# Two-source forms for VectorE's small operations, parameter rows set up at tile 8, splits written behind the products, output transposes at the end of the delta-net chain

## The chip, the cores and the metric

The kernel runs on one core of one Trainium2 chip. The metric is the device time of one execution in microseconds (us), as the median of some runs. Times inside a run are read from one profiled execution. Engines: PE is TensorE, DVE is VectorE, ACT is ScalarE, POOL is GpSimd, SP is SyncE (here it only issues DMAs).

## The reference, cut to what matters

One layer of a hybrid decoder on 256 tokens of width 1024 in float32, with 16 learned meta tokens ahead of them (272 positions):

```python
h = layer_norm(concat(meta, x))                   # 272 x 1024
proj = h @ w_in                                   # 1024 x 5640: q,k,v | z | beta, a | sb q,k,v | two gates of 1024
A = gated_delta_net(conv_silu(q, k, v), beta, g)  # 4 heads of 128, then rms_norm(o) * silu(z)
B = stick_breaking(sq, sk, sv)                    # 8 heads of 64
h = LN1(alpha*h + W_out(sig(gA)*W_A(A) + sig(gB)*W_B(B)))
h = LN2(alpha*h + HierMoE(h))                     # top-1 of 4 groups, top-2 of its 8 experts, FF 256
```

All of it is float32 in and out. The kernel writes each float32 matrix as a high and a low half (tiles of type fp32r) and makes three products of them.

## The kernel before, in words

**Stages.** To 24 us the embeddings are normalised and transposed; hTh and hTl (L213 to L217) are the halves of their transpose, `[128, 8, 272]`. From 15 to 235 us runs the projection with the two mixers woven into it. Then come the branch products, w_out, LN1 and the router (to about 323 us), then 32 experts whose weights stream from HBM (to about 525 us), and LN2.

**The projection.** `project` (L250) goes over 44 column tiles of w_in, each 128 columns wide. I number them 0 to 43 in the order of work. For each tile `load_split` (L224) issues a 512 KB DMA on SP (L231), ACT casts it to the high half (L232), and POOL subtracts to get the low half (L233; the *split*). For tiles 6, 8 and 10 (`DVE_SUB`) DVE does that. PE then makes 24 products (`mm3`, L237 to L239, 8 blocks of 3), and a `use` function takes the result out of PSUM (a convolution, a copy, a sigmoid gate). Raw tiles have a ring of WR = 3 buffers, split tiles one of WB = 3. Before the products of tile i, `project` writes the splits up to tile i+2 into the program.

**The chains.** While PE works through the tiles, `weave` (L63) advances other chains, written as generators, at given rates for each yield of `project` (4 yields a tile): masks; `delta_net` (the `gating` of L436, then two `local` parts, c = 0 and 1, and a meta part in turns, then `scan_state` for c = 0 and 1); `stick_breaking`; and `parameter_rows` (L824), which prepares the rows of gains and biases of the layer norms: four memsets and five affine selects on POOL (L828 to L835), 12 small DMAs on SP (L838), and operations on DVE and ACT that make `lnr`, `sel`, `RB` and `lnh` (L839 to L843). In the kernel before it waits 32 yields from tile 20 on, so it stands near tile 28 of the program. In the trace its POOL part runs at 184 us.

Inside `local`, `invert` computes the inverse of a triangular matrix by doubling: POOL makes masked copies mb4, mb8, ... of `mtf` (L488, one for each of c0, c1 and the meta part m), PE multiplies x4 = mb4 x pN, ACT casts the product to xo4 (L509), PE makes y4 and z4 from xo4 (L513, L516), DVE subtracts them. `scan_state(c)` ends in a short chain that normalises the output o: ACT squares (L710), DVE (L712 to L714), POOL a power (L715), DVE (L716), ACT scales (L718), and then PE transposes o to poT (L724), three yields after it. `pvp` (L685) is an earlier product of it that waits for DVE's vsc (L680).

**What sets the order.** PE and POOL run in exactly the order in which the program is written here. DVE, ACT and SP are put in order by a scheduler that reckons with its own times. Each engine runs its instructions strictly in that order; a waiting instruction holds up all that stand behind it.

After the projection its buffers become free, and only then do the first expert weights load (L889).

Of the kernel before, what the change touches and what calls it, by code (L numbers as in the profile page):

```python
# [78 lines left out]
def block_kernel(ctx: ExitStack, tc: tile.TileContext, io, out, dbg=None):  # L79
# [352 lines left out]
    def gating():  # L432
# [15 lines left out]
        V.tensor_scalar_add(beta, xin[:, 0, :], 1.0)  # L448
# [3 lines left out]
        V.tensor_scalar_add(zz, u, 2.0)  # L452
# [1155 lines left out]
```

## Time and profile before

| | us |
|---|---|
| median of 3 runs | 544.2 (541.4 to 544.8) |
| the profiled execution, own time | 538.66 |
| its span | 536.9 |
| mean granted TensorE clock over the span | 0.922 of full speed |
| PE busy | 463.5 (86%) |
| DVE, ACT, POOL busy | 238.2, 183.9, 172.7 |

The profiled execution is 5.5 us below the median of the three runs. Times "at 203 us" are counted from the start of its span. In the timeline a row is: start, duration, engine, line, operation, output<-input with shapes, count, and in brackets how long the engine had been idle and which engine's instruction ended that.

### The profile page before, as it was taken

The page shows a single profiled execution, that of the slowest core. Times are in us where ns is not written, and L with a number is a line of the kernel's source. Part 1 is how long each engine was busy: PE and PEld are TensorE (multiplying, and loading weights), DVE is VectorE, ACT ScalarE, POOL GpSimd, SP SyncE. Part 2 cuts the span into 40 slices and gives each one's busy share as a digit, 9 for nine tenths or more (in the row PEclk, how much of TensorE's full clock was granted, in tenths as well). Part 3 has the DMA queues.
Part 4 walks back from the last instruction along what each step waited for, and adds up shares of the span by engine and source line. Part 5 has one row for each costly group of instructions (what it writes and reads, how often), then busy time and mean ns, then how long its engine had stood idle before and what let it go on. Part 6 is the DMA issues. An engine that isn't in the chain of part 4 may idle for free. (4 is left out here: it accounts for less than half of the span.)

```text
span 536.9 us, 8673 instructions
## 1 busy us (share of the span) xinstructions
PE 463.5 (86%) x3301; PEld 328.6 (61%) x3301; DVE 238.2 (44%) x518; ACT 183.9 (34%) x382; POOL 172.7 (32%) x154
## 2 busy tenths in 40 slices
PE   7897999999999978997998888988879888667881
PEld 3697999999997877997876763533222222122330
DVE  5874645665296653039976736120220212110116
ACT  2453546436556365543443312120110202100310
POOL 6594698756544634738132100000000000000002
PEclk9697999999998997999999898889889898878886
DMA  8553344333441612797898958999999999999942
GB/s 210 126 151 86 79 117 109 89 92 108 117 110 49 159 42 78 207 305 270 306 338 336 399 234 336 419 418 418 419 420 420 417 419 418 417 415 419 410 196 79
DMA packets 74581, 136.33 MB, mean 254 GB/s; under 512 B 9857, under 2 KB 59154, under 8 KB 62242
## 3 DMA queue, kind: packets, MB, share of 16 engines
q1 hardware_dynamic: 72640, 134.26, 68.9%
q10 hardware_dynamic: 1890, 1.39, 0.8%
q8 instruction: 32, 0.52, 0.4%
q14 instruction: 19, 0.16, 0.1%
HBM read 133.54 MB, written 2.10 MB: 253 GB/s over the span
## 5 line engine op out<-in xcount | busy, mean ns | idle before, releaser
L233 POOL TENSOR_TENSOR ws_in<-wr_in,ws_in 128x1024 fp32r<-128x1024 f32 x41 | 99.4, 2429 | 64.6 <-ACT ws_in L232 64.3
L237 PE MATMUL pj<-hTh,ws_in 128*128 128x256 f32 (+1 forms) x352 | 109.3, 311 | 1.2 <-DVE hTh L213 0.7
L238 PE MATMUL pj<-hTl,ws_in 128*128 128x256 f32 (+1 forms) x352 | 103.1, 293 | 0.7 <-DVE hTl L217 0.7
L239 PE MATMUL pj<-hTh,ws_in 128*128 128x256 f32 (+1 forms) x352 | 102.6, 292 | 0.0
L1340 PE MATMUL pg<-gu,xs 128*32 128x512 f32 x640 | 77.6, 605 | 8.9 <-DMA gu<-expert_w_up 5.2
L1565 POOL TENSOR_SCALAR rs<-mv 128x1 f32<-128x1 f32 x2 | 0.4, 221 | 229.8 <-DVE mv L1564 229.8
L237 PEld LDWEIGHTS pj<-hTh,ws_in 128*128 128x128 f32 x352 | 69.2, 197 | 3.5 <-issue 1.0
L238 PEld LDWEIGHTS pj<-hTl,ws_in 128*128 128x128 f32 x352 | 69.3, 197 | 1.7 <-DVE hTl L217 1.7
L239 PEld LDWEIGHTS pj<-hTh,ws_in 128*128 128x128 f32 x352 | 69.1, 196 | 0.0
L1389 PE MATMUL py<-dn,hd 128*32 128x512 f32 x320 | 54.1, 802 | 11.9 <-DMA dn<-expert_w_down 6.9
L1340 PEld LDWEIGHTS pg<-gu,xs 128*32 128x32 f32 x640 | 31.0, 111 | 51.0 <-issue 45.5
L232 ACT CAST ws_in<-wr_in 128x1024 fp32r<-128x1024 f32 x44 | 45.9, 1044 | 3.0 <-DMA wr_in<-w_in 3.0
L1393 DVE TENSOR_TENSOR yy<-py,yy 128x512 fp32r<-128x512 f32 x20 | 13.8, 692 | 68.9 <-ACT yy L1392 61.7
L1365 DVE TENSOR_SCALAR sc<-pt,smod 128x256 fp32r<-128x256 f32 x10 | 4.8, 484 | 88.2 <-PE pt L1364 88.2
L1389 PEld LDWEIGHTS py<-dn,hd 128*32 128x32 f32 x320 | 13.2, 138 | 43.8 <-issue 27.2
L1401 PE MATMUL y<-yy,sc 128*128 128x512 f32 x80 | 24.5, 423 | 5.6 <-ACT yy L1392 3.0
L1392 ACT CAST yy<-py 128x512 fp32r<-128x512 f32 x20 | 11.7, 587 | 51.2 <-PE py L1389 51.2
L1401 PEld LDWEIGHTS y<-yy,sc 128*128 128x128 f32 x80 | 13.5, 188 | 22.7 <-ACT yy L1392 7.4
L1371 ACT ACTIVATE gs<-pg 128x256 f32<-128x256 f32 x10 | 3.8, 384 | 68.7 <-PE pg L1340 68.7
L314 DVE SCALAR_TENSOR_TENSOR qkv<-pj,cols,qkv 128x271 f32<-128x271 f32 (+2 forms) x36 | 17.9, 497 | 9.9 <-ACT qkv L312 9.2
L955 POOL TENSOR_TENSOR h<-h,gb 128x512 f32<-128x512 f32 x8 | 12.9, 1643 | 12.9 <-ACT gb L952 12.9
L771 DVE TENSOR_TENSOR_SCAN kp<-kp,one 128x144 f32<-128x144 f32 (+1 forms) x16 | 12.8, 842 | 7.2 <-ACT kp L766 7.2
(535 smaller groups left out, 806.6 us busy)
## 6 DMA issues: line engine op xcount, KB each, us to landing
gu<-expert_w_gate SPq DMA_DIRECT2D x32, 1024.0 KB
gu<-expert_w_up SPq DMA_DIRECT2D x32, 1024.0 KB
dn<-expert_w_down SPq DMA_DIRECT2D x32, 1024.0 KB
wr_in<-w_in SPq DMA_DIRECT2D x44, 512.0 KB
wr_o<-w_out SPq DMA_DIRECT2D x8, 512.0 KB
wr_w_branch_dn<-w_branch_dn SPq DMA_DIRECT2D x4, 512.0 KB
wr_w_branch_sb<-w_branch_sb SPq DMA_DIRECT2D x4, 512.0 KB
h<-x SPq DMA_DIRECT2D x2, 512.0 KB
```

The lines of the kernel that those rows point to most:

```text
L232: A.copy(wh, raw)
L233: (sub or V).tensor_sub(wl, raw, f32(wh))
L237: T.matmul(pt, lh, rh, start=first, stop=False)
L238: T.matmul(pt, lh, rl, start=False, stop=False)
L239: T.matmul(pt, ll, rh, start=False, stop=last)
L314: V.scalar_tensor_tensor(y[:, s:], pt[:, :L - s], ccol(3 - s, r + j), y[:, s:], op0=ALU.mult, op1=ALU.add)
L771: V.tensor_tensor_scan(k_, k_, bc(one1, [P, n]), 1.0, op0=ALU.mult, op1=ALU.mult)
L955: G.tensor_tensor(x_, x_, gb, op=op)
L1340: T.matmul(pgd[u, part][c, :], xsd[u, part][:, k, c], raw[e][0][:, :, k, :], start=k == 0, stop=k == KT - 1)
L1389: T.matmul(py[c, :], hd[(u + part) % 2][:, r, c], raw[e][1][:, r, n * 512:(n + 1) * 512], start=r == 0, stop=r == 1)
L1393: V.tensor_sub(yy[:, 1, :], py, f32(yy[:, 0, :]))
L1401: T.matmul(y[t][n], sct[(u + part) % 2][:, t * P:(t + 1) * P], yy[:, p_, :], start=False, stop=p_ == 1 and part == 0 and u == NQ - 1)
```

## The change

Four things change, and some small ones with them.

1. **Two-source forms.** Small DVE operations with one tensor source and a constant (`tensor_scalar`, `tensor_copy`) become `scalar_tensor_tensor` with a second tensor of zeros (or of a constant) through a helper `with_scalar`. This covers the six casts of hTh (L213), and operations on 128x9 or 128x4 elements in `gating`, `local`, `meta` and `scan_state`. Two copies (kTm, vTm) go to ACT. The tag `gtmp` gets three buffers in place of two.
2. **Parameter rows.** `parameter_rows` is started with the weave of tile 8 on, so that its memsets, selects and DMAs are written at tile 8; then it yields 100 times before the operations on DVE and ACT.
3. **Splits.** `project(i)` writes splits up to tile i+1 ahead of the products of tile i, and the split of tile i+2 behind the last product and the `use` of tile i.
4. **Output transposes.** poT and what follows it are taken out of `scan_state` and put into `out_turned(c)`, which runs for both c after the whole scan.

```diff
@@ prologue
+    def with_scalar(out, x, a, op):
+        V.scalar_tensor_tensor(out, x, a, bc(zero[:x.shape[0]], ...), op0=op, op1=ALU.add)
         if k % 4:
             A.activation(hf, pt[:, :L], AF.Identity, bias=bcol(k), scale=gcol(k))
-            V.tensor_copy(hTh[:, k, :], hf)
+            with_scalar(hTh[:, k, :], hf, 0.0, ALU.add)
@@ project
-            while len(split) < min(i + WB, len(todo)):
-                c = todo[len(split)][0]
-                split.append(load_split(...))
+            splits(i + WB - 1)
...
                 if k == KT - 1:
                     use(pt, j)
+                    splits(i + WB)
                     project.i += 1
@@ gating (and seven more of this kind)
-        V.tensor_scalar_add(beta, xin[:, 0, :], 1.0)
+        with_scalar(beta, xin[:, 0, :], 1.0, ALU.add)
@@ scan_state
         for h in range(HD):
             A.activation(o[:, h, :], o[:, h, :], AF.Copy, scale=sso[:, h:h + 1])
-        yield
-        yield
-        yield
+        os_.append(o)
+        yield
+    def out_turned(c):
+        o = os_[c]
         poT = v4(ps("gd", f"poT{c}"))
@@ delta_net
         for c in range(2):
             yield from scan_state(c, st, boxes[c])
+            yield
+        for c in range(2):
+            for _ in range(3):
+                yield
+            yield from out_turned(c)
@@ parameter_rows
-        for _ in range(32):
-            yield
         G.memset(f32(RB), 0.0)
...
+        for _ in range(100):
+            yield
         V.tensor_scalar(lnr, lnr, asc, None, op0=ALU.mult)
         A.copy(sel, self_)
@@ the weaves
+    prow = parameter_rows()
     weave(project(8), (mk, 0.375), (dn, R1))
-    weave(project(8), (dn, R1))
+    weave(project(8), (dn, R1), (prow, 1.0))
...
-    weave(project(20), (svc, 1.0), (dn, R3), (sbr, R4), (parameter_rows(), 1.0))
+    weave(project(20), (svc, 1.0), (dn, R3), (sbr, R4), (prow, 1.0))
+    drain(prow)
```

The lines of the kernel after are shifted: L232 and L233 become L243 and L244, L488 and L509 become L504 and L525, L715 becomes L731, L724 becomes L745, L841 becomes L867.

What this moves on the engines, at four places. First ACT, at tiles 11 to 13, before: `ws_in0` and `ws_in128` are the weights of tiles 12 and 13, `skT` copies of tiles 10 and 11, `pNc` and `xo4` belong to the inverse.

```order
L344 COPY skT_264<-pj2824_889 128x272
L232 CAST ws_in128_928<-wr_in128_927 128x1024
L500 CAST pNc1_868<-i0c1_921 128x512
L500 CAST pNm_880<-i0m_939 64x64
L509 CAST xo4c0_955<-x4c0_950 128x512
L509 CAST xo4c1_970<-x4c1_965 128x512
```

The same place on ACT after:

```order
L360 COPY skT_270<-pj2824_890 128x272
L243 CAST ws_in128_981<-wr_in128_980 128x1024
L516 CAST pNc1_869<-i0c1_927 128x512
L516 CAST pNm_886<-i0m_940 64x64
L866 CAST sel_99<-self__100 56x24
L525 CAST xo4c0_956<-x4c0_951 128x512
L525 CAST xo4c1_971<-x4c1_966 128x512
```

The scheduler has put the cast of `sel`, which reads POOL's `self_`, ahead of the casts xo4; `RB<-lnr` follows five rows later, ahead of the convolution of tile 12.

Second, POOL from the same tiles on, before (`ws_in2952` is the split of tile 11, `ws_in0` of 12, `ws_in128` of 13, `ws_in256` of 14).

```order
L233 TENSOR_TENSOR ws_in2952_819<-wr_in2952_818,ws_in2952_819 128x1024
L488 TENSOR_TENSOR mb4c0_859<-mtf0_812,off4_252 128x512
L488 TENSOR_TENSOR mb4c1_870<-mtf1_835,off4_252 128x512
L488 TENSOR_TENSOR mb4m_882<-mtfm_847,off4_252 64x64
L233 TENSOR_TENSOR ws_in0_885<-wr_in0_884,ws_in0_885 128x1024
L233 TENSOR_TENSOR ws_in128_928<-wr_in128_927,ws_in128_928 128x1024
L488 TENSOR_TENSOR mb8c0_948<-mtf0_812,off8_253 128x512
L488 TENSOR_TENSOR mb8c1_963<-mtf1_835,off8_253 128x512
L488 TENSOR_TENSOR mb8m_979<-mtfm_847,off8_253 64x64
L233 TENSOR_TENSOR ws_in256_986<-wr_in256_985,ws_in256_986 128x1024
```

POOL after (the row ahead of these is, in both, the second vs of L636):

```order
L504 TENSOR_TENSOR mb4c1_871<-mtf1_836,off4_258 128x512
L244 TENSOR_TENSOR ws_in2952_881<-wr_in2952_880,ws_in2952_881 128x1024
L504 TENSOR_TENSOR mb4m_888<-mtfm_848,off4_258 64x64
L244 TENSOR_TENSOR ws_in0_923<-wr_in0_922,ws_in0_923 128x1024
L504 TENSOR_TENSOR mb8c0_949<-mtf0_818,off8_259 128x512
L504 TENSOR_TENSOR mb8c1_964<-mtf1_836,off8_259 128x512
L244 TENSOR_TENSOR ws_in128_981<-wr_in128_980,ws_in128_981 128x1024
L504 TENSOR_TENSOR mb8m_985<-mtfm_848,off8_259 64x64
L852 MEMSET RB_96 56x256
L853 MEMSET self__100 56x24
L854 MEMSET lnr_97 56x256
L857 AFFINE_SELECT self__100<-self__100 56x24 x2
```

Each split has slipped behind one step of the inverse, and the rows' memsets and the selects that finish `self_` stand behind the split of tile 13 and mb8m.

Third, POOL near tile 29 (`ws_in3720`), before; `sso0` is the power of L715 for c = 0.

```order
L233 TENSOR_TENSOR ws_in3592_1899<-wr_in3592_1898,ws_in3592_1899 128x1024
L233 TENSOR_TENSOR ws_in3720_1986<-wr_in3720_1985,ws_in3720_1986 128x1024
L715 TENSOR_TENSOR sso0_2033<-sso0_2033,mhalf_114 128x4
L233 TENSOR_TENSOR ws_in3848_2060<-wr_in3848_2059,ws_in3848_2060 128x1024
L233 TENSOR_TENSOR ws_in3976_2104<-wr_in3976_2103,ws_in3976_2104 128x1024
```

and after:

```order
L244 TENSOR_TENSOR ws_in3592_1998<-wr_in3592_1997,ws_in3592_1998 128x1024
L731 TENSOR_TENSOR sso0_2065<-sso0_2065,mhalf_120 128x4
L244 TENSOR_TENSOR ws_in3720_2092<-wr_in3720_2091,ws_in3720_2092 128x1024
L244 TENSOR_TENSOR ws_in3848_2136<-wr_in3848_2135,ws_in3848_2136 128x1024
L244 TENSOR_TENSOR ws_in3976_2204<-wr_in3976_2203,ws_in3976_2204 128x1024
```

The split of tile 29 now stands behind the power of c = 0; before, it stood ahead of it.

Fourth, PE around the two transposes poT before (`pj3720` is tile 29, `pj4488` tile 35, `pz4` and `po2` belong to the stick-breaking chain).

```order
L239 MATMUL pj3720_2108<-hTh_175,ws_in3720_1986 128x256
L724 MATMUL poT0_2127<-ident_105,o0_1970 128x128 x4
L759 MATMUL pz4_2136<-skT_264,sqT_263 128x144
...
L239 MATMUL pj4488_2494<-hTh_175,ws_in4488_2358 128x256
L724 MATMUL poT1_2507<-ident_105,o1_2345 128x128 x4
L800 MATMUL po2_2516<-wT4_2457,sv0_265 64x256
```

and after (`pj4872` is tile 38):

```order
L250 MATMUL pj4488_2481<-hTh_181,ws_in4488_2428 128x256
L745 MATMUL poT0_2494<-ident_105,o0_2007 128x128 x4
L826 MATMUL po2_2503<-wT4_2444,sv0_271 64x256
...
L250 MATMUL pj4872_2627<-hTh_181,ws_in4872_2579 128x256
L745 MATMUL poT1_2640<-ident_105,o1_2276 128x128 x4
L248 MATMUL pj4872_2627<-hTh_181,ws_in4872_2579 128x256
```

The transpose of c = 0 stands six tiles later, that of c = 1 three tiles later.

## Rows read from the trace of the kernel before

**Rows 1.** The page: busy time by engine (share of the span, instructions).

```profile
PE 463.5 (86%) x3301; PEld 328.6 (61%) x3301; DVE 238.2 (44%) x518; ACT 183.9 (34%) x382; POOL 172.7 (32%) x154
```

**Rows 2.** Busy time by engine in stretches: start:end, length, busy (and instructions) of PE, of PE's weight loads, DVE, ACT, POOL, then the granted TensorE clock as a share of full speed, the DMA's share and GB/s.

```profile
130.00:150.00 20.00, 20.00 (x164) 18.61 (x163) 7.53 (x16) 11.89 (x28) 10.01 (x6) 1.00 0.42 110
150.00:225.00 75.00, 67.94 (x538) 60.70 (x537) 41.67 (x75) 39.81 (x93) 37.56 (x25) 0.93 0.37 96
325.00:500.00 175.00, 142.57 (x984) 51.24 (x987) 29.32 (x80) 25.48 (x58) 0.00 (x0) 0.88 1.01 418
```

**Rows 3.** What PE waited for over the whole run: its line, whom it waited for, us in total, times, the longest.

```profile
PE poT L724 <- ACT o L718: 5.8, 2, 4.6
...
PE pdc L469 <- DVE gg L464: 3.4, 1, 3.4
...
PE pvp L685 <- DVE vsc L680: 1.2, 1, 1.2
```

**Rows 4.** Stretches around those waits, columns as in rows 2.

```profile
47.40:53.30 5.90, 5.76 (x27) 5.72 (x28) 1.70 (x5) 1.56 (x4) 0.99 (x1) 0.50 0.30 86
...
166.60:167.90 1.30, 0.09 (x2) 0.06 (x1) 0.76 (x1) 0.51 (x2) 0.74 (x1) 1.00 0.00 0
...
169.70:173.00 3.30, 3.30 (x17) 2.55 (x16) 2.50 (x3) 3.20 (x8) 2.25 (x1) 0.52 0.27 81
...
180.00:182.00 2.00, 0.75 (x7) 0.55 (x5) 2.00 (x7) 1.41 (x2) 0.83 (x2) 1.00 0.18 16
198.40:203.00 4.60, 0.05 (x1) 0.00 (x0) 3.17 (x6) 1.59 (x6) 3.32 (x2) 1.00 0.00 0
...
203.80:210.60 6.80, 6.80 (x36) 5.43 (x37) 3.09 (x3) 3.18 (x7) 2.35 (x1) 0.51 0.56 151
```

**Rows 5.** The timeline of POOL, DVE, ACT and PE ahead of the transpose for c = 1.

```profile
199.20 1.02 POOL L715 TENSOR_TENSOR sso<-sso,mhalf 128x4 f32<-128x4 f32 x1 [6.92 <-ACT wT L788]
200.20 2.33 POOL L233 TENSOR_TENSOR ws_in<-wr_in,ws_in 128x1024 fp32r<-128x1024 f32 x1
200.25 2.30 DVE L716 TENSOR_TENSOR sso<-sso,rq 128x4 f32<-128x4 f32 x1 [1.01 <-POOL sso L715]
...
202.59 1.28 ACT L718 ACTIVATE o<-o,sso 128x128 f32<-128x128 f32 x4 [3.01 <-DVE sso L716]
203.04 1.35 PE L724 MATMUL poT<-ident,o 128*128 128x128 f32 x4 [4.59 <-ACT o L718]
```

**Rows 6.** The timeline around the power for c = 0: POOL's split of tile 29 and the power, PE's first product of tile 29; between them all scans of the stick-breaking chain on DVE, with columns as in rows 7 (the longest begins at 155.6).

```profile
155.39 2.81 POOL L233 TENSOR_TENSOR ws_in<-wr_in,ws_in 128x1024 fp32r<-128x1024 f32 x1 [2.91 <-ACT ws_in L232]
...
L771 DVE TENSOR_TENSOR_SCAN kp<-kp,one x16: 443/692/2836, 146.8 to 194.1; 128x144 f32<-128x144 f32 x8, 128x272 f32<-128x272 f32 x8
...
163.98 1.01 POOL L715 TENSOR_TENSOR sso<-sso,mhalf 128x4 f32<-128x4 f32 x1 [5.79 <-DVE sso L714]
...
164.34 0.28 PE L237 MATMUL pj<-hTh,ws_in 128*128 128x256 f32 x1
```

**Rows 7.** DVE beside POOL: the casts of hTh and the subtractions of hTl (durations in ns: least, median, longest; first and last start), and then the timeline row of beta.

```profile
L213 DVE CAST hTh<-hf x6: 294/296/2443, 16.1 to 21.8; 128x272 fp32r<-128x272 f32 x6
...
L217 DVE TENSOR_TENSOR hTl<-hf,hTh x8: 431/440/1267, 14.9 to 22.4; 128x272 fp32r<-128x272 f32 x8
...
42.07 0.94 DVE L448 TENSOR_SCALAR beta<-xin 128x9 f32<-128x9 f32 x1 [2.48 <-ACT xin L446]
```

**Rows 8.** The timeline of POOL from the second `vs` on (the split at 64.11 is that of tile 11, the two at 71.67 are those of tiles 12 and 13), then that of the rows' POOL part.

```profile
62.14 2.04 POOL L636 TENSOR_TENSOR vs<-ssk,half 128x4 f32<-128x4 f32 x2 [3.10 <-DVE ssk L631]
64.11 2.73 POOL L233 TENSOR_TENSOR ws_in<-wr_in,ws_in 128x1024 fp32r<-128x1024 f32 x1
66.81 4.63 POOL L488 TENSOR_TENSOR mb4c<-mtf,off 128x512 fp32r<-128x512 f32 x2
...
71.67 4.73 POOL L233 TENSOR_TENSOR ws_in<-wr_in,ws_in 128x1024 fp32r<-128x1024 f32 x2
76.36 2.53 POOL L488 TENSOR_TENSOR mb8c<-mtf,off 128x512 fp32r<-128x512 f32 x2
78.84 0.33 POOL L488 TENSOR_TENSOR mb8m<-mtfm,off 64x64 fp32r<-64x64 f32 x1
...
184.05 0.31 POOL L828 MEMSET RB<- 56x256 f32 x1
...
184.66 0.47 POOL L833 TENSOR_SCALAR_AFFINE_SELECT self__100<-self__100 56x24 f32<-56x24 f32 x2
```

**Rows 9.** The timeline of PE and ACT at the first step of the inverse (the first row is PE's first product of tile 11), and of SP's small DMAs of the rows (first and last) and DVE's row that follows them.

```profile
70.75 0.37 PE L237 MATMUL pj<-hTh,ws_in 128*128 128x272 f32 x1
...
73.31 0.59 ACT L509 CAST xo4c<-x4c 128x512 fp32r<-128x512 f32 x1 [0.81 <-PE x4c L507]
...
76.25 0.56 PE L513 MATMUL y4c<-xo4c,pTc 128*128 128x128 f32 x4
...
84.26 0.56 PE L513 MATMUL y8c<-xo8c,pTc 128*128 128x128 f32 x4
...
184.69 0.69 SPq L838 DMA_DIRECT2D lnr<-ln_g  x2
...
188.97 0.64 SPq L838 DMA_DIRECT2D lnr<-ln_emb_b  x2
...
195.96 0.34 DVE L839 TENSOR_SCALAR lnr<-lnr,asc 56x256 f32<-56x256 f32 x1
```

More of the change, by code (lines that the diff above doesn't have):

```diff
@@ L138, in block_kernel @@
     V.memset(one1, 1.0)
+    zero = ht.tile([P, 1], F32, name="zero")
+    V.memset(zero, 0.0)
+    pcol = ht.tile([P, 1], F32, name="pcol")
+    V.memset(pcol, float(P))
+    ecol = ht.tile([P, 1], F32, name="ecol")
+    V.memset(ecol, RMS_EPS)
+    def with_scalar(out, x, a, op):
+        V.scalar_tensor_tensor(out, x, a, bc(zero[:x.shape[0]], list(x.shape)) if len(x.shape) == 2 else bc(zero[:x.shape[0], :, None], list(x.shape)), op0=op, op1=ALU.add)
     half = ht.tile([P, HD], F32, name="half")
@@ L245, in columns, with splits @@
         todo.extend((c0 + j * P, n0, use, j) for j in range(n // P))
+    def splits(n):
+        while len(split) < min(n, len(todo)):
+            c = todo[len(split)][0]
+            split.append(load_split(w_in[:, :, c:c + P], f"in{c}", sub=V if len(split) in DVE_SUB else G))
     def project(n):
@@ L250, in project @@
             i = project.i
-            while len(split) < min(i + WB, len(todo)):
-                c = todo[len(split)][0]
-                split.append(load_split(w_in[:, :, c:c + P], f"in{c}", sub=V if len(split) in DVE_SUB else G))
+            splits(i + WB - 1)
             c, n0, use, j = todo[i]
@@ L438, in gating @@
         xin = mx.tile([P, 3, 9], F32, name="xin")
-        V.tensor_scalar_mul(xin[:, 0, :], bb, -1.0)
+        with_scalar(xin[:, 0, :], bb, -1.0, ALU.mult)
         V.scalar_tensor_tensor(xin[:, 1, :], aa, -1.0, aa, op0=ALU.mult, op1=ALU.min)
@@ L447, in gating @@
         u, eal = xin[:, 1, :], xin[:, 2, :]
[L448 removed]
+        with_scalar(beta, xin[:, 0, :], 1.0, ALU.add)
         V.reciprocal(beta, beta)
         zz = mx.tile([P, 9], F32, name="zz")
[L452 removed]
+        with_scalar(zz, u, 2.0, ALU.add)
         V.reciprocal(zz, zz)
@@ L457, in gating @@
         poly = mx.tile([P, 9], F32, name="poly")
-        V.tensor_scalar_mul(poly, z2, 1.0 / 17.0)
+        with_scalar(poly, z2, 1.0 / 17.0, ALU.mult)
         for d in (15, 13, 11, 9, 7, 5, 3):
@@ L461, in gating @@
         V.scalar_tensor_tensor(poly, poly, 1.0, zz, op0=ALU.add, op1=ALU.mult)
-        V.tensor_scalar_mul(poly, poly, 2.0)
+        with_scalar(poly, poly, 2.0, ALU.mult)
         V.scalar_tensor_tensor(poly, aa, 0.0, poly, op0=ALU.max, op1=ALU.add)
@@ L474, in gating @@
         A.activation(decm, pdc[:64, 24:25], AF.Exp)
-        V.tensor_scalar_mul(nedec, dec[:, 0, :], -1.0)
+        with_scalar(nedec, dec[:, 0, :], -1.0, ALU.mult)
         yield
@@ L544, in meta @@
         vTm = mx.tile([P, 64], F32, name="vTm")
-        V.tensor_copy(kTm.rearrange("p (h t) -> p h t", h=HD), qkv[:, 4:8, :NM])
+        A.copy(kTm.rearrange("p (h t) -> p h t", h=HD), qkv[:, 4:8, :NM])
         yield
@@ L551, in meta @@
         vsm = mx.tile([64, 1], F32, name="vsm")
-        V.tensor_scalar_add(ssm, ssm, RMS_EPS)
+        with_scalar(ssm, ssm, RMS_EPS, ALU.add)
         G.tensor_tensor(vsm, ssm, half[:64, :1], op=ALU.pow)
@@ L583, in meta @@
             yield "idle"
-        V.tensor_copy(vTm.rearrange("p (h t) -> p h t", h=HD), qkv[:, 8:12, :NM])
+        A.copy(vTm.rearrange("p (h t) -> p h t", h=HD), qkv[:, 8:12, :NM])
         yield
@@ L607, in local @@
         tag = ("gd", "sb")[c]
-        Aall = mx.tile([P, HD, P], F32, name=f"Aall{c}", tag="gtmp", bufs=2)
+        Aall = mx.tile([P, HD, P], F32, name=f"Aall{c}", tag="gtmp", bufs=3)
         gc = gg[:, 4 * c:4 * c + 4]
@@ L617, in local @@
         A.activation(E, pD, AF.Exp)
-        Es = mx.tile([P, HD, P], F32, name=f"Es{c}", tag="gtmp", bufs=2)
+        Es = mx.tile([P, HD, P], F32, name=f"Es{c}", tag="gtmp", bufs=3)
         V.tensor_mul(Es, E, bc(lt_[:, None, :], [P, HD, P]))
@@ L630, in local @@
             V.tensor_mul(kd, pk, bc(esuf(c)[:, :, None], [P, HD, P]))
-        V.tensor_scalar_add(ssk, ssk, RMS_EPS)
+        with_scalar(ssk, ssk, RMS_EPS, ALU.add)
         s = mx.tile([P, HD], F32, name=f"s{c}")
@@ L655, in local @@
             A.activation(junk(), pq[:, h, :], AF.Square, accum_out=rq[:, h:h + 1])
-        V.tensor_scalar(rq, rq, RMS_EPS, float(P), op0=ALU.add, op1=ALU.mult)
+        V.scalar_tensor_tensor(rq, rq, RMS_EPS, bc(pcol, [P, HD]), op0=ALU.add, op1=ALU.mult)
         G.tensor_tensor(rq, rq, mhalf, op=ALU.pow)
@@ L691, in scan_state @@
             T.matmul(pqS[:, h, :], qT(h)[:, tok], St[:, h, :], start=True, stop=True)
-        o = mx.tile([P, HD, P], F32, name=f"o{c}", tag="gtmp", bufs=2)
+        o = mx.tile([P, HD, P], F32, name=f"o{c}", tag="gtmp", bufs=3)
         for h in range(HD):
@@ L713, in scan_state @@
         V.tensor_mul(sso, sso, rq)
-        V.tensor_scalar(sso, sso, 1.0 / P, RMS_EPS, op0=ALU.mult, op1=ALU.add)
+        V.scalar_tensor_tensor(sso, sso, 1.0 / P, bc(ecol, [P, HD]), op0=ALU.mult, op1=ALU.add)
         G.tensor_tensor(sso, sso, mhalf, op=ALU.pow)
@@ L718, in scan_state @@
             A.activation(o[:, h, :], o[:, h, :], AF.Copy, scale=sso[:, h:h + 1])
+        os_.append(o)
         yield
-        yield
-        yield
+    os_ = []
+    def out_turned(c):
+        o = os_[c]
         poT = v4(ps("gd", f"poT{c}"))
@@ L724, in scan_state @@
             T.transpose(poT[:, h, :], o[:, h, :], ident)
-        of = mx.tile([P, HD, P], F32, name=f"of{c}", tag="gtmp", bufs=2)
+        of = mx.tile([P, HD, P], F32, name=f"of{c}", tag="gtmp", bufs=3)
         V.tensor_mul(of, poT, zT[:, :, c * P:(c + 1) * P])
```

## The prediction

> **What bounds the kernel now.** I read the page's busy times first. PE is busy for 86% of the span and no other engine for more than 44% [rows 1]. The table by stretches tells where that holds: in quiet tiles of the projection PE is busy all the time at full clock; from 150 to 225 us it is idle for 7 us and its granted clock is 0.93; from 325 to 500 us the DMA's share is 1.01 at 418 GB/s and PE has time over [rows 2]. So the projection is bound by PE and its waits, and the experts by HBM. The change touches the projection. The experts' weights can only load when the projection's buffers are free, so I carry a microsecond won or lost in the projection to the end one for one.
>
> The list of PE's waits then names what can be won: two waits at the output transposes poT (4.6 and 1.2 us), one of 1.2 us at pvp, and one of 3.4 us at pdc, in the gating [rows 3]. A wait costs more than its length. After the 4.6 us from 198.4 on, PE worked for 6.8 us at a granted clock of 0.51, the lower level (1.2 of 2.4 GHz); after the 1.3 us at 166.6 it had 0.52 for 3.3 us; after the wait at pdc 0.50 for 5.9 us. After the wait at pvp the stretch to 182 shows 1.00 [rows 4]. So the price of the clock is 0.49 x 6.8 = 3.3 us, 0.48 x 3.3 = 1.6 us, 0.50 x 5.9 = 2.9 us, and nothing.
>
> **Output transposes.** Ahead of poT for c = 1 stands a chain: the power on POOL, 1.02 us; then DVE's L716, a product of 128x4 elements that takes 2.30 us because it starts beside a split of 2.33 us and ends with it; then ACT's scaling, and PE [rows 5]. None of this gets shorter, but PE now asks for it six tiles later (c = 0) and three tiles later (c = 1). A quiet tile takes 24 x 20.0 / 164 = 2.9 us [rows 2], so three give 8.8 us, more than the 4.6 us missing. I take both waits as gone with their clock: 4.6 + 3.3 + 1.2 + 1.6 = 10.7 us. The transposes and the work behind them on DVE and ACT stay. The wait at pvp came of vsc standing behind other work on DVE; pkS for c = 1, which feeds it, moves ahead of the scores pz, so I take its 1.2 us as won too (bounds 0 and 1.2). Gain: 11.9 us.
>
> **Two-source forms.** L716 has two sources in SBUF and was held for a whole split [rows 5]. The single-source cast of hTh was held too (2443 ns where the median is 296), and so was beta with its one tensor (0.94 us) [rows 7]. The rows give no reason for one form to escape where the other does not. So beta stays late, and the wait at pdc of 3.4 us with it, which in any case follows the exponentials on ACT. I take 0 there; if the form did escape, up to 0.8 us of beta. In the prologue the six casts of 0.295 us become operations like the subtraction of hTl, 0.44 us [rows 7]: +0.15 us each, 0.9 us on DVE, which PE follows closely in tile 0; I take +0.6 us, with bounds of -2.1 (the long cast is freed, 2.44 - 0.3) and +0.9.
>
> The Trainium skill, page "SBUF — State Buffer", section "Who interferes with whom", states that a DVE instruction with two SBUF inputs contends with a GpSimd instruction that reads SBUF, and that the shared port pair is an exclusive lock held for the whole instruction. L716 agrees: 2.30 us beside a split of 2.33. By that rule the edit goes the wrong way: each new form that meets a split where the old one did not would wait for up to 2.3 us. By the rows above the old forms were held already, so my sum has no such term.
>
> **Parameter rows.** This is the largest loss. In ACT's new order the cast of sel stands ahead of the casts xo4, and it waits for POOL's self_. On POOL the memsets and selects stand behind both mb4c, the splits of tiles 11, 12 and 13, mb4m, mb8c and mb8m. POOL had no idle time from 62.14 to 79.17 us [rows 8], and the same work in another sequence ends at the same time, about 79.2. Then come the memsets and the selects of self_: from 184.05 to 184.66 + 0.47 they took 1.08 us [rows 8]. So self_ is ready at about 80.3. The bounds are 78.1 (both mb4c as quick as mb8c, 2.1 us less) and 81.4 (one more step slow by as much as half a split). Then come sel, which is small (I put 0.2 us), and xo4 with 0.59 us [rows 9]: PE can start y4c at 81.1. It asked for it at 76.25 [rows 9], and a little later in the new kernel, since tile 11 is late: 76.5. PE waits 4.6 us (2.4 to 5.7). Nothing else stands in PE's order that it could do first. The clock should fall as after the waits of 3.4 and 4.6 us: +2.9 us, or 1.6 after the shortest. Loss: 7.5 us (4.0 to 9.0).
>
> Later on ACT the cast RB waits for DVE's row on lnr, and that for the 12 small DMAs on SP. They can start after the memset of lnr, about 80, and their issue took 184.69 to 189.61, 4.9 us [rows 9]. The last lands between that and DVE's row at 195.96, 6.3 us later [rows 9]; I take 2 us, nearer to the short end since DVE had other work ahead of that row. That is 87, when PE, late itself, is just finishing tile 12: no further wait. Where they stood before, PE did not wait for them, so nothing is won there. SP is held for those 4.9 us; the weights of tile 17 behind them are wanted more than ten us later.
>
> **Splits.** The split of tile 11 goes behind both mb4c: instead of 64.11 to 66.84 it runs from 68.7 to 71.1 or 71.5 [rows 8], and PE's first product of tile 11 was at 70.75 [rows 9]; the low half is needed by the third product. +0.4 us (0 to 0.8).
>
> The split of tile 29 ended at 158.2; now it stands behind the power for c = 0, which started at 163.98, while PE starts tile 29 at 164.34 [rows 6]. By these times the split ends at 163.98 + 1.01 + 2.3 = 167.3 and PE waits 2.8 us. But the split used to hold a scan on DVE in that chain for 2.84 us where the median is 0.69 [rows 6]: without it the power comes up to 2.1 us earlier, and the wait is 0.7. I take 1.4 us, in between but nearer to the short one, and 0.8 us of clock by half of the 1.6 behind the 1.3 us wait (0 to 1.6). Loss 2.2 us (0.7 to 4.4). The wait for poT of c = 0 that stood 2 us later is then simply replaced. The power of c = 1 now stands ahead of the split of tile 34, two full tiles or 5.8 us behind the product that its chain follows, with other products between; the power and the split take 3.4 us of it [rows 5], so I expect no wait.
>
> **Sum.** -11.9 + 0.6 + 7.5 + 0.4 + 2.2 = -1.2 us, so the profiled execution of 538.66 us becomes about 537.5. That one lies 5.5 us below the median of 544.2, and I take the difference over as it is: 543.0 us. Within 1% (5.4 us) is about what a measurement of this kernel can tell from no change. Own range of this case: with the bounds of the two large losses, 538.0 to 546.7.
>
> **Rivals.**
> - *sel is ready in time, so only the gains stay.* If the POOL work ahead of it shrinks, or ACT's wait falls where PE has other work, the 7.5 us go: 543.0 - 7.5 = 535.5 us. For it: mb4c took 4.63 us where mb8c of the same shape took 2.53, so POOL can be quicker here. Against: even that leaves 2.4 us of wait and a loss of 4.0, giving 539.5, and POOL shows no gap. Half the loss together with no wait at tile 29 gives 537.3, faster by over 1%.
> - *The rows make PE wait twice.* If the small DMAs land 6.3 us after their issue, DVE's row on lnr ends at 91.6, RB at 92.0, and behind it on ACT stand the convolution of tile 12, the cast of tile 15 and xo8, three operations of at least 0.59 us like xo4, some 2.1 us: 94.1. PE reached y8c 8.0 us after y4c (84.26 against 76.25) [rows 9], with the lower clock behind the wait about 11: 92.2. It waits 2 us, with 1.6 us of clock: 546.6 us. It decides from a landing of about 4.4 us on; each us later costs one more. With the upper ends of sel (+1.5) and of tile 29 (+2.2) it passes 549.6, slower by over 1%. For it: the order in which these stand; against: small transfers on a DMA that is less than half used in this stage.
> - *Two-source forms escape POOL's splits.* The long cast and beta run free, up to 0.8 + 2.1 + 0.6 = 3.5 us: 539.5. Against it is L716.
> - *The change does not remove the poT waits*, because something else of the delta-net chain ends as late: 543.0 + 7.9 = 550.9. Against: nothing in PE's order between tiles 31 and 38 needs that chain but poT.
>
> **How the numbers follow.** My case 0.45; sel in time or nearly so 0.27; rows twice 0.13; two-source forms 0.08; poT waits stay 0.07. Faster by over 1% (below 538.8): most of the second, a third of the fourth, a little of mine, 0.32. Slower by over 1%: half of the third, nearly all of the fifth, a little of mine, 0.18. Same: 0.50. The range of 8 in 10 leaves out the ends: 533 to 551.
>
> **What would show it.** After the change the list of waits has no poT row, and the stretch near 204 to 210 shows full clock. There is a new wait of 4 to 5 us at y4c for ACT's xo4, ACT idle ahead of sel for POOL's self_ near 80 us, and a granted clock of 0.5 behind it. There is a wait of 1 to 3 us at tile 29's second product for POOL's split. Beta still takes over 0.5 us, and pdc waits over 2.5 us. I am wrong if y4c waits less than 2 us, if another wait of over 3 us appears, or if the projection's end moves by more than 4 us.

## The result and the profile after

| | before | after |
|---|---|---|
| median of 20 runs, us | 540.4 (538.4 to 544.8) | 545.6 (542.5 to 553.7) |
| ratio, 95% interval | | 1.0103 (1.008 to 1.0126) |
| span of the profiled execution | 536.9 | 544.1 |

With more runs the median of before is 540.4, not the 544.2 of the first three; ratios below are against runs of before on the same chip. One run of the changed kernel, 553.7 us, lies far above the others and is not in the ratio. The kernel became 1% slower where I forecast 0.2% faster: a small miss in size, but the sign was wrong, and two of my terms, the transpose for c = 1 and the prologue, were far out. That 545.6 lies within 0.5% of my 543.0 is luck in part: my number stood on the 544.2, and with the same sum on 540.4 it would have been 539.2.

PE's waits after, as in [rows 3] (its line, whom it waited for, us in total, times, longest):

```profile
PE y4c L529 <- ACT xo4c L525: 4.0, 1, 4.0
...
PE pdc L485 <- DVE gg L480: 3.9, 1, 3.9
...
PE po L831 <- DVE wTm L816: 3.8, 1, 3.8
...
PE pj L250 <- POOL ws_in L244: 1.6, 2, 1.1
```

The poT waits are gone, y4c is there with about the length forecast (4.0 us for 4.6), and there is one of over 3 us that I had not named: po. To see what each costs with its clock, take the start of each tile's first product from PE's timeline and subtract that of before. The steps in this shift are the terms of the sum. Each row is from one profiled execution, in us:

| tile | 3 | 8 | 12 | 13 | 14 | 29 | 30 | 35 | 36 | 43 | end of span |
|---|---|---|---|---|---|---|---|---|---|---|---|
| after, us | 2.8 | 3.8 | 4.5 | 12.5 | 13.1 | 13.0 | 11.6 | 9.5 | 7.3 | 8.2 | 7.2 |
| rows back | 1.9 | 2.7 | 3.5 | 3.5 | 3.4 | 3.5 | 2.0 | -0.1 | -7.4 | -7.2 | -8.0 |
| wTm on ACT | 2.6 | 3.6 | 4.3 | 12.5 | 12.9 | 12.9 | 11.4 | 9.3 | 1.5 | 1.9 | 3.4 |
| product c = 1 on POOL | 1.8 | 2.5 | 3.2 | 10.3 | 10.7 | 10.6 | 9.2 | 7.1 | 2.9 | 3.2 | 2.3 |
| sel on POOL | 2.8 | 2.2 | 2.9 | 2.9 | 10.0 | 10.9 | 9.4 | 7.3 | 4.3 | 5.1 | 4.1 |
| transposes back | 2.5 | 1.9 | 2.6 | 9.5 | 9.8 | 9.8 | 7.8 | 11.4 | 8.2 | 8.0 | 9.9 |
| transposes alone | 1.2 | 1.7 | 1.7 | 1.7 | 1.7 | 1.7 | -1.1 | 3.9 | -3.9 | -3.8 | -1.6 |
| rows alone | 1.2 | 0.1 | 0.1 | 0.1 | 4.9 | 7.1 | 5.7 | 13.1 | 11.6 | 12.3 | 12.2 |
| late splits alone | 1.1 | 2.0 | 2.7 | 2.7 | 2.7 | 2.7 | 0.8 | 1.2 | -1.3 | -1.6 | -2.0 |
| best | 1.5 | 2.0 | 2.0 | 2.0 | 2.0 | 2.0 | -0.9 | -2.7 | -10.5 | -10.4 | -8.4 |

(The lower rows belong to the experiments; "back" is one part of the changed kernel undone, "alone" one part on the kernel before.) The first place is tiles 11 to 13. The timeline of POOL and ACT after, which answers to [rows 8, 9]:

```profile
70.49 2.61 POOL L504 TENSOR_TENSOR mb4c<-mtf,off 128x512 fp32r<-128x512 f32 x1 [0.76 <-DVE mtf L660]
73.06 2.38 POOL L244 TENSOR_TENSOR ws_in<-wr_in,ws_in 128x1024 fp32r<-128x1024 f32 x1
...
80.49 2.34 POOL L244 TENSOR_TENSOR ws_in<-wr_in,ws_in 128x1024 fp32r<-128x1024 f32 x1
82.79 0.31 POOL L504 TENSOR_TENSOR mb8m<-mtfm,off 64x64 fp32r<-64x64 f32 x1
83.05 0.30 POOL L852 MEMSET RB<- 56x256 f32 x1
...
83.66 0.47 POOL L857 TENSOR_SCALAR_AFFINE_SELECT self__100<-self__100 56x24 f32<-56x24 f32 x2
...
84.15 0.21 ACT L866 CAST sel<-self__100 56x24 fp32r<-56x24 f32 x1 [7.48 <-POOL self__100 L857]
84.27 1.06 ACT L525 CAST xo4c<-x4c 128x512 fp32r<-128x512 f32 x2
```

ACT stands still for 7.48 us ahead of a cast of 0.21 us, and xo4 stands behind it. The second place is the chain that ends at po, in order of time:

```profile
196.79 1.02 POOL L731 TENSOR_TENSOR sso<-sso,mhalf 128x4 f32<-128x4 f32 x1 [4.71 <-ACT osh L834]
197.76 2.38 POOL L244 TENSOR_TENSOR ws_in<-wr_in,ws_in 128x1024 fp32r<-128x1024 f32 x1
197.84 2.32 DVE L732 TENSOR_TENSOR sso<-sso,rq 128x4 f32<-128x4 f32 x1 [1.19 <-POOL sso L731]
200.19 1.28 ACT L734 ACTIVATE o<-o,sso 128x128 f32<-128x128 f32 x4 [3.45 <-DVE sso L732]
...
202.68 0.50 ACT L792 ACTIVATE kp<-pz 128x416 f32<-128x416 f32 x1
...
203.22 2.95 DVE L797 TENSOR_TENSOR_SCAN kp<-kp,one 128x144 f32<-128x144 f32 x2 [2.72 <-ACT kp L792]
205.78 4.92 POOL L244 TENSOR_TENSOR ws_in<-wr_in,ws_in 128x1024 fp32r<-128x1024 f32 x2 [0.55 <-ACT ws_in L243]
206.09 4.90 DVE L798 TENSOR_TENSOR sg<-sg,kp 128x127 f32<-128x127 f32 x2
...
212.61 0.47 DVE L816 COPY wTm<-pw 64x128 f32<-64x128 f32 x2
212.94 0.67 PE L831 MATMUL po<-wTm,svm 64*64 64x128 f32 x2 [3.75 <-DVE wTm L816]
```

The same held product of 128x4 as in [rows 5] no longer delays poT, which is wanted later. It delays ACT's scaling, and behind that on ACT stand the scores kp; DVE's work on them starts late, two splits hold it for 4.9 us, and behind it on DVE stand the copies wTm, which PE needs. Both waits cost the clock too, as in [rows 4]:

```profile
80.90:84.90 4.00, 0.01 (x2) 0.00 (x1) 0.00 (x0) 0.75 (x3) 3.64 (x11) 1.00 0.27 71
84.90:92.00 7.10, 7.10 (x33) 6.79 (x34) 3.21 (x7) 1.76 (x4) 5.11 (x4) 0.53 0.43 119
...
209.20:212.90 3.70, 0.00 (x0) 0.00 (x0) 3.70 (x9) 0.00 (x0) 1.51 (x1) 0.82 0.78 203
212.90:219.60 6.70, 6.66 (x38) 6.33 (x38) 1.90 (x4) 2.76 (x5) 0.97 (x1) 0.59 0.15 44
```

After the wait PE has 0.53 for 7 us, and 0.59 for 6.7 us: some 3 us each.

### The profile page after: what moved, and what is told of

It reads as the page before. It is cut to its first block, busy times and chain, and to the rows that moved or that the text cites. A ratio compares the mean times of both kernels' runs of the same rounds, so it can differ in the third digit from the quotient of the medians.

```text
span 544.1 us, 8672 instructions
## 1 busy us (share of the span) xinstructions
PE 461.3 (85%) x3301; PEld 330.3 (61%) x3301; DVE 239.9 (44%) x519; ACT 184.4 (34%) x384; POOL 170.0 (31%) x154
## 5 line engine op out<-in xcount | busy, mean ns | idle before, releaser
L244 POOL TENSOR_TENSOR ws_in<-wr_in,ws_in 128x1024 fp32r<-128x1024 f32 x41 | 98.9, 2418 | 63.2 <-ACT ws_in L243 58.3
L248 PE MATMUL pj<-hTh,ws_in 128*128 128x256 f32 (+1 forms) x352 | 110.9, 315 | 0.0
L249 PE MATMUL pj<-hTl,ws_in 128*128 128x256 f32 (+1 forms) x352 | 104.7, 297 | 1.4 <-DVE hTl L228 1.4
L250 PE MATMUL pj<-hTh,ws_in 128*128 128x256 f32 (+1 forms) x352 | 104.5, 297 | 1.6 <-POOL ws_in L244 1.6
L1368 PE MATMUL pg<-gu,xs 128*32 128x512 f32 x640 | 79.3, 614 | 15.3 <-DMA gu<-expert_w_up 8.0
L249 PEld LDWEIGHTS pj<-hTl,ws_in 128*128 128x128 f32 x352 | 70.7, 201 | 2.3 <-DVE hTl L228 2.3
L248 PEld LDWEIGHTS pj<-hTh,ws_in 128*128 128x128 f32 x352 | 70.7, 201 | 2.1 <-issue 1.0
L250 PEld LDWEIGHTS pj<-hTh,ws_in 128*128 128x128 f32 x352 | 70.7, 201 | 2.1 <-POOL ws_in L244 2.1
L1368 PEld LDWEIGHTS pg<-gu,xs 128*32 128x32 f32 x640 | 29.1, 113 | 61.1 <-issue 55.0
L1417 PE MATMUL py<-dn,hd 128*32 128x512 f32 x320 | 46.6, 715 | 11.9 <-DMA dn<-expert_w_down 6.9
L243 ACT CAST ws_in<-wr_in 128x1024 fp32r<-128x1024 f32 x44 | 46.0, 1045 | 2.6 <-DMA wr_in<-w_in 2.6
L1417 PEld LDWEIGHTS py<-dn,hd 128*32 128x32 f32 x320 | 10.7, 126 | 38.9 <-issue 24.3
L330 DVE SCALAR_TENSOR_TENSOR qkv<-pj,cols,qkv 128x271 f32<-128x271 f32 (+2 forms) x36 | 17.9, 497 | 11.3 <-ACT qkv L328 10.7
L1408 ACT COPY hd<-pt 128x256 f32<-128x256 f32 x10 | 3.7, 373 | 32.4 <-PE pt L1407 32.4
```

The lines of the kernel that those rows point to most:

```text
L243: A.copy(wh, raw)
L244: (sub or V).tensor_sub(wl, raw, f32(wh))
L248: T.matmul(pt, lh, rh, start=first, stop=False)
L249: T.matmul(pt, lh, rl, start=False, stop=False)
L250: T.matmul(pt, ll, rh, start=False, stop=last)
L330: V.scalar_tensor_tensor(y[:, s:], pt[:, :L - s], ccol(3 - s, r + j), y[:, s:], op0=ALU.mult, op1=ALU.add)
```

## The experiments

**One part undone.** Four kernels are the changed one with one of its parts as before (in one of them the two-source helper is replaced by the old `tensor_scalar` and `tensor_copy` calls). The rows first:

```diff
-    weave(project(8), (dn, R1), (prow, 1.0))
+    weave(project(8), (dn, R1))
...
-    weave(project(20), ..., (prow, 1.0))
+    weave(project(20), ..., (parameter_rows(), 1.0))   # 32 yields ahead of its memsets again
```

Expected: 

> The changed kernel with the parameter rows back in their old place, all else as changed. My theory: of the changed kernel's loss, the 8.0 us between tiles 12 and 13 come of one thing, the cast of sel that ACT runs ahead of xo4 and that waits for POOL's self_. Then the wait at y4c (4.0 us) and the low clock behind it go, tile 13 starts with a shift of about +4 us against before, and the time is about 0.995 of before (1.010 - 8.0/540). Rival: POOL is overfull at tiles 11 to 14 because the splits now stand behind the inverse's steps, and PE waits there all the same for a split: 1.005 or more, with a wait of over 2 us at tile 13 or 14 for POOL.

Measured: 0.9839 (0.9816 to 0.9862), 531.0 us. The wait at y4c is gone, but the gain is 14 us and not 8. The table shows where the rest is: at tile 36 the shift falls from -0.1 to -7.4. Those 7.3 us are nearly the whole of the 7.9 us that I had forecast for poT of c = 1; of the wait at po 0.3 us is left. The timeline there shows why:

```profile
187.18 1.02 POOL L731 TENSOR_TENSOR sso<-sso,mhalf 128x4 f32<-128x4 f32 x1 [4.70 <-ACT osh L834]
188.15 0.31 POOL L854 MEMSET RB<- 56x256 f32 x1
...
188.23 0.16 DVE L732 TENSOR_TENSOR sso<-sso,rq 128x4 f32<-128x4 f32 x1 [1.19 <-POOL sso L731]
...
191.56 3.72 DVE L797 TENSOR_TENSOR_SCAN kp<-kp,one 128x144 f32<-128x144 f32 x2 [2.83 <-ACT kp L792]
...
199.57 0.47 DVE L816 COPY wTm<-pw 64x128 f32<-64x128 f32 x2
```

With the rows here, POOL has memsets and selects behind the power where it would start a split: the product takes 0.16 us, not 2.32. From the product to the copies wTm it is 11.3 us, not 14.8.

Splits ahead of the products again: 

> The changed kernel with the splits written ahead of the products again, all else as changed. Built that way the scheduler puts the cast of sel behind xo4 and the cast of tile 14. My theory: the wait at y4c comes only of the two edits together, so it goes here too (-8 us), and with it the 0.8 us at tile 11 and the 1.1 us at tile 29: 0.992 of before. Rival: the rows' set-up on POOL at tile 13 costs PE by itself, by a late split or a late RB: 1.003 or more.

Measured: 1.0038 (1.0009 to 1.0068). The rival's number came. In the profile, taken of its longest run (547.0 us), y4c is no wait any more, yet tiles 13 to 15 lose 7.7 us all the same, since DVE's row on lnr waits for the small DMAs, with the subtractions of y8 behind it:

```profile
90.84 0.34 DVE L864 TENSOR_SCALAR lnr<-lnr,asc 56x256 f32<-56x256 f32 x1 [4.23 <-DMA lnr<-ln_emb_b]
91.11 0.67 DVE L532 TENSOR_TENSOR pNc<-pNc,y8c 128x512 fp32r<-128x512 f32 x1
```

Transposes back: 

> The changed kernel with the transposes poT back in scan_state, all else as changed. My theory: moving them has won the waits at poT and brought a new one at po of 3.8 us, net about 5 us between tiles 29 and 36; undone, the poT waits of 1 and 4 to 5 us are back with their clock and the one at po goes: 1.010 + 0.008 = 1.018 of before. Rival: the two waits have one cause, DVE held beside POOL's splits, and moving the transposes only renamed it: 1.010, no more than 0.003 away.

Measured: 1.0182 (1.0149 to 1.0215), my theory's number, but not by its waits. The wait at po is gone, but none at poT is back: PE waits 1.8 us at pvp and, ahead of poT for c = 1, for a split that now stands behind the same power:

```profile
208.22 1.01 POOL L731 TENSOR_TENSOR sso<-sso,mhalf 128x4 f32<-128x4 f32 x1 [16.32 <-ACT wT L804]
209.20 4.68 POOL L244 TENSOR_TENSOR ws_in<-wr_in,ws_in 128x1024 fp32r<-128x1024 f32 x2
...
211.60 0.58 PE L250 MATMUL pj<-hTh,ws_in 128*128 128x256 f32 x1 [2.88 <-POOL ws_in L244]
```

So the move won about 4 us even with the new wait (tile 29 to 36: -5.7 against -1.6), against other waits than those of the kernel before.

Single-source forms again: 

> The changed kernel with the single-source forms on DVE again, all else as changed. My theory: the prologue's +2.8 us come mostly of h's normalisation on DVE held beside the first split (2.98 us where it is 0.8), a matter of when the data of x land, and only 0.9 us of the six longer casts; the poly's operations are equally held in either form: 1.008 of before, tile 3 about 1 us earlier than in the changed kernel when h is not held. Rival: the two-source forms cost all of the prologue's 2.8 us and the 1.0 us at tile 8 as well: 1.003.

Measured: 1.0138 (1.0094 to 1.0182). Neither: no gain at all. In its profile tile 3 starts 2.2 us earlier than in the changed kernel's, but the projection ends only 0.7 us earlier.

**One part alone, on the kernel before.** Transposes: 

> The kernel before with the output transposes moved and nothing else. Here, too, the split of a projection tile stands right behind the power of c = 1. My theory: the poT waits go (-4.6 -3.3 -1.2 -1.6 us, and -1.2 at pvp), and a wait at po of 2 to 4 us with its clock takes the place of the larger one: 0.988 to 0.992 of before. Rival: the po wait of the changed kernel belongs to the other edits, and all of the 11.9 us comes: 0.978.

Measured: 0.9876 (0.9805 to 0.9947), the theory's number, but without its wait: there is none at po, though the product behind the power is held here too (2.33 us). In its place PE waits earlier:

```profile
PE pqv L710 <- DVE vt L691: 2.9, 1, 2.9
```

DVE's vt stands behind scores held 4.93 us by two splits. That and its clock cost 4.5 us at tile 31, and PE comes to po later by them.

Rows: 

> The kernel before with the parameter rows set up at tile 8 and nothing else. The scheduler puts sel behind xo4 here and DVE's row on lnr ahead of the subtractions behind y8. My theory: the rows cost by themselves, by DVE waiting for the small DMAs ahead of those subtractions: PE waits 3 to 6 us near y8 and z8 with its clock, +7.7 us, and no gain later: 1.014 of before. Rival: the rows cost only together with the splits (the sel cast), 1.000 to 1.004.

Measured: 1.0137 (1.0053 to 1.0221). DVE waited 4.19 us for the DMAs, and tiles 13 to 15 lost 7.0 us. The rows cost by themselves. The profiled execution (550.8 us) lost another 7.5 us at tiles 31 and 32, in a wait of 4.9 us at pvp: POOL ran two splits without a gap, and DVE's scores ahead of vsc were held by both:

```profile
181.28 5.04 POOL L233 TENSOR_TENSOR ws_in<-wr_in,ws_in 128x1024 fp32r<-128x1024 f32 x2 [1.07 <-ACT ws_in L232]
181.66 4.94 DVE L776 TENSOR_TENSOR sg<-sg,kp 128x127 f32<-128x127 f32 x2
...
190.72 2.07 PE L689 MATMUL pvp<-vsc,tTc 128*128 128x128 f32 x8 [4.86 <-DVE vsc L684]
```

In the kernel before, the same work took 2.74 us there. Whether the rows bring this about, or only the times at which PE and ACT arrive there, no run shows.

Two-source forms and late splits, as two kernels. The forms: 

> The kernel before with the two-source forms on DVE and nothing else. My theory now: they cost the 1.5 us by which tile 3 starts later in the eight profiles that have them than in the six that do not (2.3 against 0.8 us behind the first profile of before), more than the 0.6 us of my prediction, and nothing after tile 3: 1.003 of before, projection's end +1 to +2 us. Rival: no effect that can be told from the scatter of the prologue: 1.000, tile 3 within 1.2 us.

The splits: 

> The kernel before with the splits written behind the products and nothing else. My theory: they cost the 0.5 us more at pdc, 0.8 us at tile 11 and 1.1 us with a part of the clock at tile 29, while the poT waits stay: 1.003 to 1.006 of before. Rival: a later split keeps POOL free for the chains and the kernel gets faster: 0.997.

Measured: forms 1.0008 (0.9976 to 1.004), splits 0.9971 (0.9939 to 1.0004). In the first tile 3 is 1.9 us late, past the rival's 1.2, but tile 8 only 0.7, and the projection's end 0.6. In the second the rival's number came: the splits cost nothing that can be measured. But that is a balance. My theory's costs are there (2.7 us at tile 12, 1.1 of it from the prologue), but its premise that the poT waits stay was wrong: neither is left, and in place of the larger one PE waits 3.5 us, at tile 35, for a split behind the power:

```profile
202.02 0.39 PE L239 MATMUL pj<-hTh,ws_in 128*128 128x256 f32 x1 [3.52 <-POOL ws_in L233]
```

From tile 29 to 36 the late splits alone win 4.0 us.

**The wait at po.** Three edits, each on its own:

```diff
-        V.tensor_mul(sso, sso, rq)                  # behind the power
+        (G if c else V).tensor_mul(sso, sso, rq)    # product, c = 1 on POOL
...
-                V.tensor_copy(wTm, pw[:64, 3 * P:4 * P])
+                A.copy(wTm, pw[:64, 3 * P:4 * P])   # wTm on ACT
...
-        A.copy(sel, self_)
+        G.tensor_copy(sel, self_)                   # sel on POOL, right behind the selects of self_
```

Product on POOL: 

> The changed kernel in which, for c = 1 alone, the 128x4 product behind the power runs on POOL, right behind the power, and not on DVE; nothing else moves on any engine. My theory: the wait at po (3.8 us and its clock) has its root in that product, which was held 2.32 us on DVE by the split that POOL starts behind the power, and then held ACT, the scores and the copies wTm in turn; in the changed kernel the split has moved up to the power because the rows' memsets and selects no longer stand between. Then the wait at po is under 1.5 us and tile 36 starts 4 to 7 us earlier: 0.998 of before. Rival: the wait comes of DVE's scan and subtractions of tile 33's scores held by two splits in a row (4.9 us), whatever stands ahead: wait at po still over 2.5 us, 1.008.

Measured: 1.0057 (1.0029 to 1.0084), between the two. The wait at po fell from 3.8 to 2.0 us, and tile 36 gained 2.0 us against tile 35 (-4.2 after -2.2). So the held product explains about half of the wait. With the rest stand the scores, which two splits still hold (0.59 us where no split runs):

```profile
201.91 2.79 DVE L798 TENSOR_TENSOR sg<-sg,kp 128x127 f32<-128x127 f32 x2
...
205.71 2.75 DVE L798 TENSOR_TENSOR sg<-sg,kp 128x127 f32<-128x127 f32 x2
```

Both theories were half right.

wTm on ACT: 

> The changed kernel with the copies wTm, which po waits for, on ACT and not on DVE. They need only the transposes pw, not the scores that stand ahead of them on DVE. My theory: the wait at po is DVE's queue: its operations on the scores of tile 33, which start late and are held by splits, stand ahead of the copies. Then no wait over 0.7 us at po, tile 36 starts 4.5 to 5.5 us earlier against tile 35 than in the changed kernel: 1.001 of before. Rival: the chain of the scores itself is late and PE waits one step later, at pw or po of the last pair: 1.008.

Measured: 1.0016 (0.9993 to 1.0039), as expected. There is no wait at po, and from tile 35 to 36 the shift falls by 7.8 us, though the scores are held as before:

```profile
205.77 0.28 ACT L816 COPY wTm<-pw 64x128 f32<-64x128 f32 x1
...
205.93 4.93 DVE L798 TENSOR_TENSOR sg<-sg,kp 128x127 f32<-128x127 f32 x2
```

So the wait stood in DVE's queue and nowhere in the data: the copies need none of the work ahead of them.

sel on POOL: 

> The changed kernel with the cast of sel on POOL, behind self_, so that ACT has nothing to wait for ahead of xo4; the rest of every engine's order stays. My theory: the rows cost twice over and the first wait hides the second. The wait at y4c (4.0 us, with its clock 8 us) goes, and in its place PE waits 2.5 to 4 us at y8c or z8m, since RB on ACT and lnr on DVE wait for the small DMAs that land near 89.6 us: +5 to 6 us with the clock. Net -2 to -3: 1.005 of before. Rival: the sel cast was all of it, no wait over 1 us near y8c: 0.996.

The profile shows my theory's wait: y4c has none, and

```profile
PE y8c L529 <- ACT xo8c L525: 4.5, 2, 3.8
```

took its place; tile 13 is late by 2.9 us and tile 14 by 10.0. The projection ends 3 us earlier than in the changed kernel. But the time was 1.0145 (1.0128 to 1.0162), above both expectations; its profiled execution, 542.7 us, was the lowest of six. The four slowest (547.2 to 548.5 us) list a mean granted clock of 0.914 to 0.917 over the span where it has 0.932; at which waits they lost it no trace shows.

**Better versions.** Transposes moved, products on POOL: 

> The kernel before with the output transposes moved and, for both c, the 128x4 product behind the power on POOL. My theory: no poT wait, and the po wait under 1.5 us, so 5 us or so less than with the transposes moved alone: 0.978 to 0.983 of before. Rival: the same as with the transposes moved alone, within 0.003.

Measured: 0.9888 (0.9819 to 0.9957); the rival. The pqv wait fell to 1.1 us, but po waited 3.9, since here the scores stood behind sel on ACT, and sel waited for POOL's self_, which stood behind a split (184.86 to 187.22):

```profile
188.27 0.21 ACT L854 CAST sel<-self__100 56x24 fp32r<-56x24 f32 x1 [1.69 <-POOL self__100 L847]
189.34 0.50 ACT L780 ACTIVATE kp<-pz 128x416 f32<-128x416 f32 x1
```

With the copies wTm on ACT and sel on POOL as well, on the kernel before: 

> The kernel before with the transposes moved, both products behind the powers and the cast of sel on POOL, and the copies wTm on ACT. My theory: all of what the moved transposes can win is won: no wait at poT or po, one of up to 1.1 us at pqv: 0.977 of before. Rival: some other wait on DVE takes their place again, 0.986 like the transposes alone.

The same three edits on the changed kernel with the rows back: 

> The changed kernel with the rows in their old place, both products behind the powers and the cast of sel on POOL, and the copies wTm on ACT. With the rows back alone there was no wait at po left. My theory: little more is to be won, 0.982 of before (0.984 with the rows back alone). Rival: the two-source forms and the late splits leave a wait of over 2 us elsewhere: 0.988.

Measured: 0.9785 (0.9756 to 0.9814), 529.2 us, on the kernel before ("best" in the table), and 0.988 (0.986 to 0.9901) on the changed one with the rows back. That is its rival's number, though its profile has no wait of over 2 us in the projection but the 3.9 at pdc, which was there without the edits; and it is no better than the rows back alone (0.9839), so there the three edits won nothing. In the first kernel, PE is busy where [rows 2] showed 7 us of idle time, at full clock:

```profile
150.00:222.00 72.00, 71.44 (x618) 66.50 (x617) 43.46 (x72) 44.78 (x107) 43.94 (x30) 1.00 0.48 134
```

## Why the prediction was wrong, step by step

- **Rows, sel: right.** Forecast 4.6 us of wait and 7.5 us in all, for ACT's xo4; measured 4.0 and 8.0 (tile 12 to 13). POOL was 4 us later than I had it and so was PE (POOL's vs began at 65.92 for 62.14 us, tile 11 was 3.7 us late), so that what I had missed ahead of them did not show in this term.
- **Rows, second wait: right as a mechanism, hidden here.** My rival of a wait at y8 is what the rows cost wherever sel does not wait first (sel on POOL, rows alone, splits back). DVE's row started 1.4 us behind the last issue of the DMAs (89.40 to 90.84 with the splits back); I had taken 2 us.
- **"Where they stood before, PE did not wait for them, so nothing is won there": wrong by omission.** Nothing was won, but something was lost: in the old place, with the other edits as they are, their POOL part keeps the split away from the power's product (0.16 us with the rows back, 2.32 in the changed kernel). The rows cost 2.6% in this company (0.9839 to 1.0103) and 1.4% alone (with a wide interval).
- **Transpose c = 1: the step that failed.** Forecast -7.9, measured -2.2 us (tile 35 to 36): the wait at poT went, and one of 3.8 us at po with its clock came in its place. I had argued against this rival that nothing in PE's order between tiles 31 and 38 needs the chain but poT. True of the data, false of the queues: po needs wTm, wTm stands behind the scores on DVE, and these behind o's scaling on ACT. I had looked at what reads o, not at what stands behind the instructions that wait for it. Where po does not wait, the forecast holds: -7.8 with wTm on ACT, -7.3 with the rows back.
- **Transpose c = 0 with the split of tile 29: right.** -0.6 forecast, -1.4 measured (tile 29 to 30): with the transposes alone it was -2.8, as I had reckoned without the split. The split's wait came (1.1 us, at tile 29's third product; my sign said the second), with the clock at 1.00 behind it.
- **pvp: right.** No wait for vsc is left.
- **Two-source forms: right that no form escapes, too small in the prologue.** Beta took 0.93 us (0.94 before), and alone the forms make 1.0008. But the prologue moved by 2.8 us where I had put 0.6, at most 0.9. The sixteen profiles of this case all but part by the forms: tile 3 starts 1.4 to 2.8 us behind that of before in the nine that have them (2.2 on the mean), 0 to 1.5 us in the seven that do not (0.8). So some 1.4 us go with the forms, and not all of it stays: alone, 1.9 us at tile 3 are 0.7 at tile 8. With one profile for each kernel, what makes the rest no run shows.
- **Late splits at pdc: not in my sum.** 3.9 us in every profile with late splits, 3.2 to 3.4 in those without; and +0.8 us at tile 11 for 0.4.

Summed by the table: prologue 2.8, gating 1.0, tile 11 0.7, sel 8.0 and 0.6 behind it, c = 0 -1.4, pvp and its neighbours -2.1, c = 1 -2.2, the rest 0.8: +8.2 us at the projection's end, against -1.2 forecast. 5.7 of these 9.4 us are the transpose of c = 1, 2.2 the prologue. The first alone does not make the sign: with wTm on ACT, where that term came out as forecast, the projection still ends 1.9 us late and the ratio is 1.0016, no gain.

## What to carry to other kernels

A wait moved away by asking later is only gone when every queue that waits for the same chain can pass too: follow, on each engine, what stands behind the waiting instruction, and who waits for that. An instruction whose data are long there (a copy, a cast of a constant) is a cheap thing to move to an engine where nothing waits ahead of it; two such moves and the products on POOL took the kernel with the transposes moved from 0.9876 to 0.9785, some 5 us, but won nothing where no such wait was left. A ratio that comes out as expected does not show the expected wait: in two of the experiments (transposes back, transposes alone) the number was right and PE waited elsewhere. And when set-up work is taken out of a place, ask what it kept apart there.
